# TensorE's order in the recurrence stage of a hybrid decoder layer, written by hand in pairs of tiles

## The chip, the cores and the metric

One core of one Trainium2 chip runs the whole program. The metric is the device time of one execution in microseconds (us), and the time of a kernel is the median of its runs. Engine names are those of the profile: PE is TensorE's matrix multiply, PEld its weight load, DVE is VectorE, ACT is ScalarE, POOL is GpSimd, SP is the engine that issues most DMAs.

## The reference

The layer takes x (1024 tokens by 1024 channels, float32), normalises it and multiplies it by one wide weight matrix; the columns of the product feed two branches. The attention branch scores keys with a small indexer, keeps the best 256 keys of each token (top-k), and does softmax attention over those. The recurrence branch is the part that the change touches:

```python
h = rg_lru(causal_depthwise_conv(x_rnn, conv_w, conv_b), w_rg_a, b_rg_a, w_rg_x, b_rg_x, lru_lambda)
y_rnn = (h * jax.nn.silu(g_rnn)) @ w_rnn_proj
```

where rg_lru computes, with 16 blocks of 64 channels (xb is x by blocks):

```python
r = jax.nn.sigmoid(jnp.einsum('bsgi,gij->bsgj', xb, w_a).reshape(B, S, C) + b_a)
i = jax.nn.sigmoid(jnp.einsum('bsgi,gij->bsgj', xb, w_x).reshape(B, S, C) + b_x)
log_a = -LRU_C * r * jax.nn.softplus(-lam)
a = jnp.exp(log_a)
b_in = jnp.sqrt(-jnp.expm1(2.0 * log_a)) * (i * x)
h_t = a_t * h_{t-1} + b_in_t        # an associative scan over the tokens
```

Both branches are weighted by sigmoid gates (merge), added, multiplied by w_out, added to x and normalised.

## The kernel before, in words

Everything is held with channels on the 128 partitions and tokens along the free axis, in 8 tiles of 128 channels by 1024 tokens. Each float32 operand of a product is split into a high and a low part (`split`, L93 to L95: ACT writes the high part, POOL or DVE the difference), and a product is three matrix multiplies: high by high, high by low, low by high (`proj_steps`, L115 to L125). One projection of one tile is 2 halves of 512 tokens, each 8 steps of 3 multiplies, so 48 multiplies; weights come by `load_w` (L105): two DMAs of 256 KB, then ACT and POOL split them. The accumulators of projections come from a ring of PSUM banks (`zt`); the gate products have two banks of their own (`tt`, tag "t").

The stages, in the order in which they are written:

- The score stage (L318 to L384): the indexer's scores, matrix multiplies `s`, ACT's Relu and DVE's weighting into `sc`. PE's order is written by hand there (`manual_schedule`, L357).
- The recurrence (`recurrence`, L447 to L528), for tiles of channels in the groups (0, 1), (2, 3), (4, 5), (6,), (7,). For every tile of a group: the projection `z_xr` (L478), copied to `xr` by ACT (L479); the convolution `xc`, four DVE instructions (L482, L484); the split `xs` of each half of 64 partitions, ACT and POOL (L490); the gate products `rg` of two multiplies for each half e and each 512 tokens (L495, L496), and ACT's two sigmoids of each (L499, with the time of L455). Then for every tile of the group the projection `z_gr` of the output gate, with ACT's Tanh and a DVE instruction into `sg` (L509, L510). Then the tail: ACT's Exp, Tanh, Square and Sqrt (L517 to L524), DVE's L520, L525, the scan L526 and L527, and the DMA of `u_r` to memory (L528). The helper `apart` with `turn` holds ACT's Sigmoids, Exps and Sqrts in batches, since each batch may need a table load. `xs` has one buffer for each e; `r`, `ig`, `sg`, `xc` and others have two.
- The merge gates `z_mr` of tiles 0 to 3 (L600), then the projections `z_rp` of the recurrence's result, read back as `urh` and `url` (L608 to L611), in alternation with the merge gates of tiles 4 to 7 (L612 to L622). DVE multiplies each half product into `grm` (L616).
- `topk` (L531 to L584), written after all that: a bisection of 31 rounds, each with 6 counting passes over `sc` (L541) and two tiny instructions (L551, L553), all on DVE; and at the end a chain for each of 6 blocks of rows, DVE's L579 to L583 and POOL's L584, through one buffer each of `eq` and `pre`.
- The attention stage (from L640), PE's order written by hand, in buffers that overlie those of `topk`; then the output projection.

The program is ordered by a scheduler that simulates the engines: on each engine it issues, among the instructions that it takes to be ready, the one that is written first. So before the change PE's order from L394 to L622 was the scheduler's, and it mixed the stages: `z_xr` of tile 0 between the scores, gate products between projections, `z_mr` between the gate products of tiles 6 and 7. DVE's order is the scheduler's everywhere; the counting passes of `topk`, written last, fill whatever time it believes to be free. On the chip each engine goes through its fixed order and waits where an operand is not there.

Of the kernel before, what the change touches and what calls it, by code (L numbers as in the profile page):

```python
# [18 lines left out]
P = 128  # L19
# [33 lines left out]
def hybrid_kernel(ctx: ExitStack, tc: tile.TileContext, x, w_b, w_a, w_ap, w_rp, w_o, vecs,  # L53
# [97 lines left out]
    with ExitStack() as p12:  # L151
# [295 lines left out]
        def recurrence(rn):  # L447
# [12 lines left out]
            for tiles in ((0, 1), (2, 3), (4, 5), (6,), (7,)):  # L460
                st = []
                turn()
                for c in tiles:
                    T = lambda nm, dt=F32, w=S: rn.tile([P, w], dt, tag=nm, name=f"{nm}{c}")
                    col = lambda v, c=c: vec[:, v + c:v + c + 1]

                    raw = rn.tile([P, 2, P], F32, tag="rgr", name=f"rgr{c}")
                    for e in range(2):
                        for u in range(2):
                            nc.sync.dma_start(raw[u * HD:(u + 1) * HD, e].rearrange("p (t d) -> p t d", t=2),  # L470
                                              w_rg[c, e * HD:(e + 1) * HD])
                    rgh = rn.tile([P, 2, P], F32R, tag="rgh", name=f"rgh{c}")
                    rgl = rn.tile([P, 2, P], F32R, tag="rgl", name=f"rgl{c}")
                    split(rgh, rgl, raw)
                    xr = T("xr", w=S + 3)
                    nc.gpsimd.memset(xr[:, 0:3], 0.0)
                    w = load_w(w_b[G_XR + c], f"xr{c}")
                    for c0, n, acc in proj(w, xhl, f"xr{c}"):  # L478
                        nc.scalar.activation(xr[:, 3 + c0:3 + c0 + n], acc, AF.Copy)  # L479
                    xc = T("xc")  # L480
                    cw = lambda k, c=c: vec[:, V_CW + 4 * c + k:V_CW + 4 * c + k + 1]
                    nc.vector.tensor_scalar(xc, xr[:, 0:S], cw(0), col(V_CB), op0=ALU.mult, op1=ALU.add)  # L482
                    for k in range(1, 4):
                        nc.vector.scalar_tensor_tensor(xc, xr[:, k:k + S], cw(k), xc, op0=ALU.mult, op1=ALU.add)  # L484

                    xs = [rn.tile([P, S], F32R, tag=f"xs{e}", name=f"xs{e}_{c}", bufs=1) for e in range(2)]
                    gates = [T("r"), T("ig")]
                    for e in range(2):
                        a, b = slice(e * HD, (e + 1) * HD), slice((1 - e) * HD, (2 - e) * HD)
                        split(xs[e][a], xs[e][b], xc[a])  # L490
                        bias = vec[:, V_BG + 2 * c + e:V_BG + 2 * c + e + 1]
                        for c0, n in chunks(S):
                            cs = slice(c0, c0 + n)
                            acc = tt(f"rg{c}_{e}_{c0}")
                            nc.tensor.matmul(acc, rgh[:, e], xs[e][:, cs], start=True, stop=False)  # L495
                            nc.tensor.matmul(acc, rgl[:, e], xs[e][:, cs], start=False, stop=True)  # L496
                            for u, dst in enumerate(gates):
                                f = slice(u * HD, (u + 1) * HD)
                                apart(dst[a, cs], acc[f], AF.Sigmoid, bias=bias[f])  # L499
                    r, ig = gates  # L500
                    nc.gpsimd.tensor_tensor(out=ig, in0=ig, in1=xc, op=ALU.mult)
                    st.append((c, r, ig))
# [84 lines left out]
        with ExitStack() as p3a:  # L587
# [10 lines left out]
            with tc.tile_pool(name="rn", bufs=2) as rn:  # L598
                recurrence(rn)
# [12 lines left out]
            for n in range(8):  # L612
# [8 lines left out]
                if n + 4 < 8:  # L621
                    merge_r(n + 4)  # L622
# [590 lines left out]
```

## Time and profile before

| | |
|---|---|
| time, median of 3 runs | 1211.18 us (1209.04 to 1211.36) |
| the profiled execution | 1213.4 us |
| its span, first to last instruction | 1211.5 us |
| mean granted clock of TensorE | 0.974 of full speed |

The profiled execution is 2.2 us above the median; 1.9 us of it lie around the span. All rows below are of that one execution; start times count from the beginning of its span. In a timeline row stand start, duration (both us), engine, line, operation, output<-inputs, shape and count; what the engine waited for before it stands in brackets.

### The profile page before, as it was taken

Reading aid. Unit: us, or ns where it says so; the run is one execution under the profiler, and the core shown is the slowest. Engines: PE = TensorE matmul, PEld = TensorE weight load, DVE = VectorE, ACT = ScalarE, POOL = GpSimd, SP = SyncE. Lnnn points to the kernel's source line nnn. Section 1 sums busy time; section 2 is a strip of 40 time slices with the busy share of each in tenths; the row PEclk is TensorE's granted clock in tenths of the full one; section 3 lists DMA queues with packets and bytes.
Section 4 is the critical chain, followed back from the end, with each engine's and each line's share of the span. In section 5 each row is a group of like instructions: output and inputs, shape, how many; then the busy total and the mean of one; then the engine's idle time right before and its main releaser. Section 6 shows DMA issues by size and latency. Waiting matters only on the chain.

```text
span 1211.5 us, 16044 instructions
## 1 busy us (share of the span) xinstructions
PE 1147.0 (95%) x5528; PEld 959.4 (79%) x5528; DVE 898.6 (74%) x1821; ACT 671.0 (55%) x1232; POOL 479.0 (40%) x383
## 2 busy tenths in 40 slices
PE   6989999897979899996999999999999998999997
PEld 5988878685858688885888888888888877888886
DVE  6777599999999999976776767676767698533335
ACT  6467558575668321114776777676667677332211
POOL 4211255445464422244443444444444435373000
PEclk8989999898989899997999999999999999999999
DMA  5110111111111532221001110111010231453322
GB/s 205 50 35 27 66 57 59 64 60 61 45 61 51 194 102 70 87 71 59 12 35 51 36 64 27 59 36 64 27 64 28 87 140 53 149 191 125 101 87 113
DMA packets 41665, 89.99 MB, mean 74 GB/s; under 512 B 4976, under 2 KB 8560, under 8 KB 41584
## 3 DMA queue, kind: packets, MB, share of 16 engines
q1 hardware_dynamic: 41440, 88.70, 21.6%
q8 instruction: 44, 0.72, 0.2%
q14 instruction: 37, 0.30, 0.1%
q10 hardware_dynamic: 144, 0.26, 0.1%
HBM read 68.49 MB, written 20.45 MB: 73 GB/s over the span
## 4 chain that ended last, share of the span: by engine, by line
PE 67%; DVE 21%; issue 4%; ACT 4%; DMA 2%; POOL 2%; SPq 0%; POOLq 0%; ACTq 0%; DVEq 0%
DVE junk L541 7%; PE pT L1048 4%; DVE xc L484 3%; PE o L1002 3%; PE l L844 3%; PE l L845 3%; PE f L113 2%; PE f L111 2%; PE f L112 2%; PE z_q L121 2%; PE z_rp L121 2%; PE z_q L123 2%; PE z_q L122 2%; PE z_rp L122 2%; PE z_rp L123 2%
## 5 line engine op out<-in xcount | busy, mean ns | idle before, releaser
L541 DVE TENSOR_SCALAR_CACHE_REDUCE junk<-sc,thr 128x384 bf16<-128x384 f32 (+2 forms) x192 | 181.1, 943 | 5.2
L1052 DVE TENSOR_TENSOR pp<-pT,pp 128x512 fp32r<-128x512 f32 (+1 forms) x160 | 100.8, 633 | 36.9 <-ACT pp L1051 35.2
L1051 ACT ACTIVATE pp<-pT 128x512 fp32r<-128x512 f32 (+1 forms) x160 | 87.8, 550 | 52.6 <-PE pT L1048 50.6
L844 PE MATMUL l<-kh,qt 128*128 128x128 f32 (+2 forms) x192 | 65.2, 342 | 10.4 <-POOL wlo_g L95 9.7
L1002 PE MATMUL o<-pp,vt 128*128 128x512 f32 x160 | 66.9, 418 | 2.1 <-DVE o L1017 1.0
L845 PE MATMUL l<-kl,qt 128*128 128x128 f32 (+2 forms) x192 | 66.2, 345 | 0.0
L852 ACT ACTIVATE l<-l,m 128x128 f32<-128x128 f32 (+4 forms) x80 | 54.0, 675 | 20.6 <-DVE m L846 20.3
L857 POOL TENSOR_SCALAR sc<-sc,m 128x384 f32<-128x384 f32 (+1 forms) x32 | 25.8, 805 | 92.7 <-DVE m L854 84.4
L1017 DVE TENSOR_TENSOR o<-o,o 64x256 f32<-64x256 f32 x128 | 53.4, 419 | 6.8 <-ACT o L1015 4.6
L349 ACT ACTIVATE r<-s 128x512 f32<-128x512 f32 (+1 forms) x80 | 39.8, 523 | 25.7 <-PE s L348 22.9
L354 DVE SCALAR_TENSOR_TENSOR sc<-r,wi,sc 128x384 f32<-128x384 f32 (+5 forms) x42 | 40.6, 999 | 18.0 <-ACT r L349 17.6
L121 PE MATMUL z_q<-xh,whi_q 128*128 128x512 f32 x128 | 53.6, 419 | 0.2 <-DVE kl L728 0.2
L121 PE MATMUL z_rp<-urh,whi_rp 128*128 128x512 f32 x128 | 51.4, 407 | 2.1 <-ACT urh L94 2.1
L122 PE MATMUL z_rp<-url,whi_rp 128*128 128x512 f32 x128 | 51.7, 404 | 1.5 <-DVE url L95 1.5
L852 ACT ACTIVATE sc<-sc,m 128x384 f32<-128x384 f32 (+2 forms) x48 | 44.9, 935 | 14.7 <-DVE m L846 13.4
L846 DVE CUSTOM_DVE_ANT_0 l<-sc,l 128x512 f32<-128x512 f16 (+3 forms) x80 | 41.3, 520 | 14.4 <-PE l L845 10.6
L844 PEld LDWEIGHTS l<-kh,qt 128*128 128x128 f32 x192 | 36.6, 191 | 19.4 <-POOL wlo_g L95 10.1
L854 DVE RECIPROCAL m<-m 128x1 f32<-128x1 f32 x128 | 20.3, 159 | 42.1 <-ACT l L852 22.8
L122 PE MATMUL z_gr<-xl,whi_gr 128*128 128x512 f32 x128 | 51.4, 401 | 0.0
L123 PE MATMUL z_rp<-urh,wlo_rp 128*128 128x512 f32 x128 | 51.3, 401 | 0.0
L121 PE MATMUL z_gr<-xh,whi_gr 128*128 128x512 f32 x128 | 51.3, 401 | 0.0
L1048 PE MATMUL pT<-ident,sc 128*128 128x128 f32 x288 | 48.9, 272 | 2.6 <-DVE pp L1052 2.6
(340 smaller groups left out, 3881.5 us busy)
## 6 DMA issues: line engine op xcount, KB each, us to landing
xt<-in_x_dram SPq DMA_DIRECT2D x8, 512.0 KB, 8.9
wraw_xr<-in_w_b_dram SPq DMA_DIRECT2D x16, 256.0 KB, 2.7
wraw_gr<-in_w_b_dram SPq DMA_DIRECT2D x16, 256.0 KB, 2.6
u_r<-ig SPq DMA_DIRECT2D x8, 512.0 KB, 2.9
wraw_mr<-in_w_b_dram SPq DMA_DIRECT2D x16, 256.0 KB, 3.2
wraw_rp<-in_w_rp_dram SPq DMA_DIRECT2D x16, 256.0 KB, 2.8
ur<-u_r SPq DMA_DIRECT2D x8, 512.0 KB, 3.2
wraw_q<-in_w_b_dram SPq DMA_DIRECT2D x16, 256.0 KB, 2.6
```

The lines of the kernel that those rows point to most:

```text
L121: nc.tensor.matmul(acc, wh, xh_, start=(k == 0), stop=False)
L122: nc.tensor.matmul(acc, wh, xl_, start=False, stop=False)
L123: nc.tensor.matmul(acc, wl, xh_, start=False, stop=(k == KT - 1))
L541: nc.vector.tensor_scalar(junk[:, :P * (b + 1)], SL(b), thr_of(b - B0), None, op0=op, op1=ALU.add, accum_out=cnt[:, b - B0:b - B0 + 1])
L844: nc.tensor.matmul(acc[:, :n], q, kh[:, c0:c0 + n], start=True, stop=False)
L845: nc.tensor.matmul(acc[:, :n], q, kl[:, c0:c0 + n], start=False, stop=True)
L852: nc.scalar.activation(l[:, :L], l[:, :L], AF.Exp, scale=-1.0, bias=mi, accum_out=m[:, 2:3])
L1002: nc.tensor.matmul(ov, vt[:, 2 * jj, :], pp[:, :, 0:256], start=(jj == 0), stop=False)
L1017: nc.vector.tensor_tensor(out=oc, in0=oacc[a:a + HD, u * 256:(u + 1) * 256], in1=oc, op=ALU.add)
L1048: nc.tensor.transpose(tp[:, k * P:(k + 1) * P], pr[u][:, j * P:(j + 1) * P], ident)
L1051: latest[:] = [nc.scalar.activation(pp[:, 0, :n], tp[:, :n], AF.Copy), nc.vector.tensor_tensor(out=pp[:, 1, :n], in0=tp[:, :n], in1=pp[:, ...
L1052: nc.vector.tensor_tensor(out=pp[:, 1, :n], in0=tp[:, :n], in1=pp[:, 0, :n].bitcast(F32), op=ALU.subtract)]
```

## The change

In `recurrence` the tiles go in four pairs, (6, 7) being one now. PE's instructions from the start of the recurrence to the last `z_rp` and `z_mr` are issued in the order in which they are written (`manual_schedule` for PE, closed ahead of `topk`). For a pair c, d that order is: `z_xr` of c, `z_xr` of d, `z_gr` of c with the gate products of c in it, `z_gr` of d with those of d in it. A projection has 16 steps of three multiplies; the four gate parts (two multiplies each) stand behind steps 6, 8, 10 and 12 (`run`: i is 5, 7, 9, 11). The splits `xs` of both halves are written ahead of all gate products. Then follow, as written, `z_mr` 0 to 3, and `z_rp` n with `z_mr` n + 4 behind it. The arithmetic of every tile is as before.

```diff
--- before.py
+++ after.py
@@ -457,63 +457,91 @@
             def turn():
                 before[:], since[:] = since, []
 
-            for tiles in ((0, 1), (2, 3), (4, 5), (6,), (7,)):
-                st = []
+            T = lambda nm, c, dt=F32, w=S: rn.tile([P, w], dt, tag=nm, name=f"{nm}{c}")
+            col = lambda v, c: vec[:, v + c:v + c + 1]
+            xss, rgw, gts, xcs, sgs = {}, {}, {}, {}, {}
+
+            def run(steps, amid=()):
+
+                amid = list(amid)
+                for i, _ in enumerate(steps):
+                    if i > 3 and i % 2 and amid:
+                        amid.pop(0)()
+                assert not amid
+
+            def inputs(c):
+
+                raw = rn.tile([P, 2, P], F32, tag="rgr", name=f"rgr{c}")
+                for e in range(2):
+                    for u in range(2):
+                        nc.sync.dma_start(raw[u * HD:(u + 1) * HD, e].rearrange("p (t d) -> p t d", t=2),
+                                          w_rg[c, e * HD:(e + 1) * HD])
+                rgh = rn.tile([P, 2, P], F32R, tag="rgh", name=f"rgh{c}")
+                rgl = rn.tile([P, 2, P], F32R, tag="rgl", name=f"rgl{c}")
+                split(rgh, rgl, raw)
+                rgw[c] = rgh, rgl
+                xr = T("xr", c, w=S + 3)
+                nc.gpsimd.memset(xr[:, 0:3], 0.0)
+
+                def evac(c0, n, acc):
+                    nc.scalar.activation(xr[:, 3 + c0:3 + c0 + n], acc, AF.Copy)
+
+                yield from proj_steps(load_w(w_b[G_XR + c], f"xr{c}"), xhl, f"xr{c}", evac)
+                xc = xcs[c] = T("xc", c)
+                cw = lambda k: vec[:, V_CW + 4 * c + k:V_CW + 4 * c + k + 1]
+                nc.vector.tensor_scalar(xc, xr[:, 0:S], cw(0), col(V_CB, c), op0=ALU.mult, op1=ALU.add)
+                for k in range(1, 4):
+                    nc.vector.scalar_tensor_tensor(xc, xr[:, k:k + S], cw(k), xc, op0=ALU.mult, op1=ALU.add)
+
+                for e in range(2):
+                    a, b = slice(e * HD, (e + 1) * HD), slice((1 - e) * HD, (2 - e) * HD)
+                    xs = xss[c, e] = rn.tile([P, S], F32R, tag=f"xs{e}", name=f"xs{e}_{c}", bufs=1)
+                    split(xs[a], xs[b], xc[a])
+                gts[c] = [T("r", c), T("ig", c)]
+
+            def gate_part(c, e, c0, n, last):
+                def go():
+                    rgh, rgl = rgw[c]
+                    xs = xss[c, e]
+                    a, cs = slice(e * HD, (e + 1) * HD), slice(c0, c0 + n)
+                    bias = vec[:, V_BG + 2 * c + e:V_BG + 2 * c + e + 1]
+                    acc = tt(f"rg{c}_{e}_{c0}")
+                    nc.tensor.matmul(acc, rgh[:, e], xs[:, cs], start=True, stop=False)
+                    nc.tensor.matmul(acc, rgl[:, e], xs[:, cs], start=False, stop=True)
+                    for u, dst in enumerate(gts[c]):
+                        f = slice(u * HD, (u + 1) * HD)
+                        apart(dst[a, cs], acc[f], AF.Sigmoid, bias=bias[f])
+                    if last:
+                        ig = gts[c][1]
+                        nc.gpsimd.tensor_tensor(out=ig, in0=ig, in1=xcs[c], op=ALU.mult)
+                return go
+
+            def gate_parts(c):
+                return [gate_part(c, e, c0, n, e and c0) for e in range(2) for c0, n in chunks(S)]
+
+            def out_gate(c):
+                sg = sgs[c] = T("sg", c)
+
+                def evac(c0, n, acc):
+
+                    nc.scalar.activation(sg[:, c0:c0 + n], acc, AF.Tanh, scale=0.5)
+                    nc.vector.scalar_tensor_tensor(sg[:, c0:c0 + n], sg[:, c0:c0 + n], 1.0, acc,
+                                                   op0=ALU.add, op1=ALU.mult)
+
+                return proj_steps(load_w(w_b[G_GR + c], f"gr{c}"), xhl, f"gr{c}", evac)
+
+            for tiles in ((0, 1), (2, 3), (4, 5), (6, 7)):
+                c, d = tiles
+                run(inputs(c))
+                run(inputs(d))
+                turn()
+                run(out_gate(c), gate_parts(c))
+                run(out_gate(d), gate_parts(d))
+                st2 = []
                 turn()
                 for c in tiles:
-                    T = lambda nm, dt=F32, w=S: rn.tile([P, w], dt, tag=nm, name=f"{nm}{c}")
-                    col = lambda v, c=c: vec[:, v + c:v + c + 1]
-
-                    raw = rn.tile([P, 2, P], F32, tag="rgr", name=f"rgr{c}")
-                    for e in range(2):
-                        for u in range(2):
-                            nc.sync.dma_start(raw[u * HD:(u + 1) * HD, e].rearrange("p (t d) -> p t d", t=2),
-                                              w_rg[c, e * HD:(e + 1) * HD])
-                    rgh = rn.tile([P, 2, P], F32R, tag="rgh", name=f"rgh{c}")
-                    rgl = rn.tile([P, 2, P], F32R, tag="rgl", name=f"rgl{c}")
-                    split(rgh, rgl, raw)
-                    xr = T("xr", w=S + 3)
-                    nc.gpsimd.memset(xr[:, 0:3], 0.0)
-                    w = load_w(w_b[G_XR + c], f"xr{c}")
-                    for c0, n, acc in proj(w, xhl, f"xr{c}"):
-                        nc.scalar.activation(xr[:, 3 + c0:3 + c0 + n], acc, AF.Copy)
-                    xc = T("xc")
-                    cw = lambda k, c=c: vec[:, V_CW + 4 * c + k:V_CW + 4 * c + k + 1]
-                    nc.vector.tensor_scalar(xc, xr[:, 0:S], cw(0), col(V_CB), op0=ALU.mult, op1=ALU.add)
-                    for k in range(1, 4):
-                        nc.vector.scalar_tensor_tensor(xc, xr[:, k:k + S], cw(k), xc, op0=ALU.mult, op1=ALU.add)
-
-                    xs = [rn.tile([P, S], F32R, tag=f"xs{e}", name=f"xs{e}_{c}", bufs=1) for e in range(2)]
-                    gates = [T("r"), T("ig")]
-                    for e in range(2):
-                        a, b = slice(e * HD, (e + 1) * HD), slice((1 - e) * HD, (2 - e) * HD)
-                        split(xs[e][a], xs[e][b], xc[a])
-                        bias = vec[:, V_BG + 2 * c + e:V_BG + 2 * c + e + 1]
-                        for c0, n in chunks(S):
-                            cs = slice(c0, c0 + n)
-                            acc = tt(f"rg{c}_{e}_{c0}")
-                            nc.tensor.matmul(acc, rgh[:, e], xs[e][:, cs], start=True, stop=False)
-                            nc.tensor.matmul(acc, rgl[:, e], xs[e][:, cs], start=False, stop=True)
-                            for u, dst in enumerate(gates):
-                                f = slice(u * HD, (u + 1) * HD)
-                                apart(dst[a, cs], acc[f], AF.Sigmoid, bias=bias[f])
-                    r, ig = gates
-                    nc.gpsimd.tensor_tensor(out=ig, in0=ig, in1=xc, op=ALU.mult)
-                    st.append((c, r, ig))
-                sgs = {}
-                for c, r, ig in st:
-                    w = load_w(w_b[G_GR + c], f"gr{c}")
-                    sg = sgs[c] = rn.tile([P, S], F32, tag="sg", name=f"sg{c}")
-                    for c0, n, acc in proj(w, xhl, f"gr{c}"):
-
-                        nc.scalar.activation(sg[:, c0:c0 + n], acc, AF.Tanh, scale=0.5)
-                        nc.vector.scalar_tensor_tensor(sg[:, c0:c0 + n], sg[:, c0:c0 + n], 1.0, acc,
-                                                       op0=ALU.add, op1=ALU.mult)
-                st2 = []
-                turn()
-                for c, r, ig in st:
-                    a = rn.tile([P, S], F32, tag="a", name=f"a{c}")
-                    sq = rn.tile([P, S], F32, tag="sq", name=f"sq{c}")
+                    r, ig = gts[c]
+                    a, sq = T("a", c), T("sq", c)
                     apart(a, r, AF.Exp, scale=nsp8[:, c:c + 1])
                     apart(r, r, AF.Tanh, scale=sp8[:, c:c + 1])
                     nc.scalar.activation(sq, a, AF.Square)
@@ -595,6 +623,8 @@
                     nc.scalar.activation(g[:, c0:c0 + m], acc, AF.Sigmoid,
                                          bias=vec[:, V_BM + 8 + n:V_BM + 9 + n])
 
+            by_hand = ExitStack()
+            by_hand.enter_context(tc.manual_schedule(engines={mybir.EngineType.PE}))
             with tc.tile_pool(name="rn", bufs=2) as rn:
                 recurrence(rn)
             for n in range(4):
@@ -620,6 +650,7 @@
                     nc.sync.dma_start(mr_d[n], g)
                 if n + 4 < 8:
                     merge_r(n + 4)
+            by_hand.close()
             topk(kp, kp2)
 
 
```

## Rows read from the trace of the kernel before

**Rows 1.** The page: busy time of each engine, and the chain that ended last

```profile
PE 1147.0 (95%) x5528; PEld 959.4 (79%) x5528; DVE 898.6 (74%) x1821; ACT 671.0 (55%) x1232; POOL 479.0 (40%) x383
...
PE 67%; DVE 21%; issue 4%; ACT 4%; DMA 2%; POOL 2%; SPq 0%; POOLq 0%; ACTq 0%; DVEq 0%
```

**Rows 2.** Busy time by stretch: length, engines' busy us, clock, DMA share, GB/s

```profile
120.00:147.40 27.40, 27.40 (x129) 22.75 (x129) 13.26 (x14) 14.28 (x28) 5.56 (x9) 1.00 0.20 68
...
166.42:280.00 113.58, 106.39 (x455) 86.54 (x454) 111.06 (x176) 75.36 (x100) 57.12 (x38) 0.97 0.17 56
280.00:400.00 120.00, 103.70 (x438) 84.10 (x437) 118.47 (x161) 81.22 (x104) 62.05 (x34) 0.93 0.19 64
400.00:503.00 103.00, 99.41 (x418) 79.70 (x417) 97.62 (x200) 26.46 (x37) 30.81 (x24) 0.97 0.33 111
503.00:555.40 52.40, 52.40 (x239) 42.92 (x238) 42.88 (x55) 5.50 (x10) 21.09 (x14) 1.00 0.23 79
...
166.42:555.40 388.98, 361.90 (x1544) 293.26 (x1543) 370.03 (x589) 188.55 (x251) 171.06 (x108) 0.96 0.23 76
```

**Rows 3.** Timeline of POOL, PE and DVE at the attention's start

```profile
555.52 2.40 POOL L584 TENSOR_TENSOR sc<-sc,eq 128x1024 f16<-128x1024 f32 x1 [3.74 <-DVE eq L582]
...
559.13 0.39 PE L123 MATMUL z_q<-xh,wlo_q 128*128 128x512 f32 x1
569.19 0.45 PE L844 MATMUL l<-kh,qt 128*128 128x128 f32 x1 [9.66 <-POOL wlo_g L95]
```

**Rows 4.** Waits of DVE, 166 to 556 us: total, times, longest us

```profile
DVE eq L579 <- POOL sc L584: 5.4, 4, 1.6
DVE grm L616 <- PE z_rp L123: 3.9, 4, 2.0
DVE url L95 <- ACT urh L94: 1.6, 2, 1.3
...
DVE grm L616 <- issue: 0.2, 1, 0.2
```

**Rows 5.** Waits of PE, 160 to 560 us: total, times, longest us

```profile
PE rg L495 <- issue: 15.8, 3, 8.2
PE rg L495 <- POOL xs L95: 7.7, 4, 4.9
PE z_rp L121 <- ACT urh L94: 2.1, 2, 1.8
PE z_rp L122 <- DVE url L95: 1.5, 2, 0.8
```

**Rows 6.** Timeline of PE: end of tile 3's z_xr, first gate product of tile 2

```profile
208.61 0.39 PE L122 MATMUL z_xr<-xl,whi_xr 128*128 128x512 f32 x1
...
210.20 0.39 PE L123 MATMUL z_xr<-xh,wlo_xr 128*128 128x512 f32 x1
...
228.82 0.80 PE L495 MATMUL rg<-xs,rgh 128*128 128x512 f32 x1 [4.86 <-POOL xs L95]
```

**Rows 7.** Timeline of ACT and POOL on tile 2's way to its gates; then tile 4's

```profile
204.86 0.58 ACT L479 ACTIVATE xr<-z_xr 128x512 f32<-128x512 f32 x1
...
224.87 2.14 ACT L94 ACTIVATE xs<-xc 64x1024 fp32r<-64x1024 f32 x2 [13.30 <-DVE xc L484]
...
290.45 1.08 ACT L509 ACTIVATE sg<-z_gr 128x512 f32<-128x512 f32 x2 [11.76 <-DVE ig L527]
```

**Rows 8.** z_xr on PE inside the score stage: length, busy us (count)

```profile
130.00:147.40 17.40, 9.35 (x36) 1.00 0.18 60
```

**Rows 9.** DVE's L551: all of them, two single ones, and a POOL split

```profile
L551 DVE TENSOR_SCALAR fail<-cnt 128x6 int32<-128x6 f32 x31 | 21.4, 689 | 0.7
...
244.98 2.36 DVE L551 TENSOR_SCALAR fail<-cnt 128x6 int32<-128x6 f32 x1
...
260.87 0.17 DVE L551 TENSOR_SCALAR fail<-cnt 128x6 int32<-128x6 f32 x1
...
244.92 2.40 POOL L95 TENSOR_TENSOR xs<-xc,xs 64x1024 fp32r<-64x1024 f32 x1
```

## The prediction

> **What bounds the kernel now.** I read the page first. PE is busy for 95% of the span and holds 67% of the chain that ended last, DVE 21% [rows 1]: two engines share the bound, so the place of the change must be looked at by itself. The windows come next. In the stretch from the first counting pass of topk to the end of DVE's last one, 166.42 to 555.40 us, DVE is busy 370.03 of 388.98 us and PE 361.90 [rows 2]. In the recurrence itself DVE has next to no gap (111.06 of 113.58 us, then 118.47 of 120.00), while PE has about 7 us of gaps in the first of these stretches and 16 in the second. So in the stage that is changed DVE is the fuller engine: whenever the recurrence does not need it, a counting pass of topk is in its queue.
>
> The timeline where the attention starts tells what ends this stage. PE finishes tile 0's query product at 559.5 us, then stands still for 9.66 us until the first logit at 569.19 [rows 3]. What that logit waited for came after POOL's last L584, which started at 555.52 and took 2.40 us: the end of topk. The attention's buffers lie over those of topk, so their copies and splits can only come behind it. Topk is DVE's chain. **The time is therefore set by the end of topk**, and a PE that is earlier helps only as far as DVE waits for PE. The waits of DVE say how far that is: 3.9 us in 4 waits of grm for z_rp and 0.2 us of issue [rows 4]; the 5.4 us for POOL's L584 are topk's own, and 1.6 are for ACT's urh.
>
> **The change, part by part.**
>
> *The written order of the gate products.* All 192 multiplies of a pair's four projections and the 16 of its gates stay, so PE's work stays. From 208.61 to 210.20 us are seven multiplies, 0.227 us each [rows 6], so a projection of 48 is 10.9 us. What changes is when PE stops for a gate product. The waits of PE give 23.5 us for the first multiply of a gate in all: 15.8 of "issue" and 7.7 for the split xs [rows 5].
>
> The 15.8 us are not a matter of xs. ACT stood 11.76 us ahead of tile 4's Tanh at 290.45 us, since the buffer sg had to wait for DVE's L527 of tile 2 [rows 7]; the sigmoids of the gates are queued behind that Tanh on ACT, and with two gate banks PE stops. The scheduler had run z_gr ahead of the gates, so the Tanh stood ahead of the sigmoids. In the new order the first two gate parts stand ahead of the first Tanh, and this wait can go. Its bounds are 0 and 15.8 us taken away.
>
> The 7.7 us can grow. Tile 2's gate is now written behind six steps of its z_gr: z_xr of tile 3 ended at 210.59 us, plus 18 multiplies of 0.227 is 214.7. Its xs came for 228.82 [rows 6], because ACT copied the second half of xr as late as 204.86 and got xc 13.30 us after its previous work [rows 7]: the tail of the pair before stood ahead on both engines. That is a wait of 14.1 us where there were 4.86; the scheduler's order had covered 9.3 of it with the rest of z_gr. Three pairs have a pair before them, so the bounds of this term are 0 (DVE's order follows the new order of PE) and 3 x 14.1 = 42.3 us.
>
> Together the waits lie between 0 and 42.3 us, where they were 23.5. I take 23.5, no change: DVE, 98 to 99% busy here [rows 2], paces both orders, and a PE that does not wait in one place waits in the next. What PE's waits cost the end is nothing so long as DVE is the fuller engine; the cover is topk's counting passes.
>
> *Pair (6, 7).* The tail of tiles 6 and 7 goes together, and four z_mr (4 x 10.9 = 43.6 us) now stand whole between the last gate and the first z_rp, where a part of them lay between the gate products. The waits of z_rp at its start, 2.1 us for urh and 1.5 for url [rows 5], should go, since tile 7 is no longer a turn later than tile 6. Bounds: 3.6 us taken away, or, if the last u_r comes later (no z_mr can now step in), as much added. I take 3.6 away. This lies on the path: from 503 us on PE is busy without a gap, 52.40 of 52.40 us [rows 2], and DVE waits for it 3.9 + 0.2 = 4.1 us [rows 4]. So of an earlier PE at most 4.1 us reach the end, and 3.6 fit in that.
>
> *z_xr out of the score stage.* Before, 36 multiplies of z_xr lay between 130 and 147.4 us [rows 8], 36 x 0.227 = 8.2 us, and PE had no gap from 120 to 147.4 while DVE was busy for only 13.26 of 27.4 [rows 2]: DVE waited for scores. If the written order keeps these out, scoring may end up to 8.2 us sooner, and DVE's full stretch begins sooner; or PE idles where they lay, and all later PE work moves back by as much. I take 0: PE had nothing else there, and the scores need PE's banks back from ACT.
>
> *Loads and queues.* No DMA, split or table load is added; the weights of z_gr are asked for ahead of the gates, as before, behind the same waits of SP and POOL. I cost them at nothing: the cover is a projection of 10.9 us for every load. If it is gone, each late weight would stop PE by itself, since no other product may step in.
>
> *DVE and POOL.* L551 is a tiny instruction: 0.17 us at 260.87, but 2.36 at 244.98, beside a POOL split that began at 244.92 and took 2.40 [rows 9]. All 31 took 21.4 us; 31 x 0.17 is 5.3, so 16.1 us of DVE's time is such meetings. The change moves every one of them and removes none. By the rows I take 0, with half of 16.1, so 8 us, as the bound either way. The Trainium skill, in "SBUF — State Buffer", section "Who interferes with whom", says that the two engines share a port pair, that the one that issues first holds it for its whole instruction, and that the other blocks. By that rule the new order alone could make DVE's chain longer with no work added; the row at 244.98 agrees.
>
> **The sum.** -3.6 us on the profiled execution: 1213.4 - 3.6 = 1209.8. That execution is 2.2 us above the median, so the forecast for the median is 1211.2 - 3.6 = 1207.6 us.
>
> **The rivals.**
>
> (a) *PE stops at the gates and falls behind DVE (slower).* Place: the first gate part of tiles 2, 4 and 6. Price: 42.3 us of waits for the 23.5 before, 18.8 more, less the 3.6 at z_rp: 15.2 us, 1226. For it: the way from z_xr to xs is 14.1 us too long for the written place [rows 6], and PE's slack at the end is none, since DVE's grm waits for z_rp already [rows 4]. Against: 15.8 us of PE's waits have another cause, which this order removes, and DVE's own order is planned anew. It decides as soon as PE's waits for gates exceed 23.5 + 3.6 us.
>
> (b) *Nothing at the end.* DVE's 4.1 us are merely replaced by longer waits for POOL's L584, since grm fills some of them today; or the planned order was as good as the written one. 1211.
>
> (c) *Scoring ends sooner too.* All 8.2 us of z_xr leave the score stage and DVE starts topk that much sooner: 1211.2 - 3.6 - 8.2 = 1199.4. For it: DVE's idle half there [rows 2]. Against: those multiplies were put where PE would have waited.
>
> (d) *More meetings of DVE and POOL.* The forecast with 8 us more on DVE: 1215.6. Nothing in the trace speaks for more rather than fewer.
>
> **How the numbers follow.** Forecast 0.40, (a) 0.20, (b) 0.20, (c) 0.12, (d) 0.08. A measurement of this kernel tells 0.2%, 2.4 us, from no change, so "same" is 1208.8 to 1213.6. Faster: nearly all of the forecast, (c), and a little of (b): 0.51. Same: most of (b) and the forecast's edge: 0.21. Slower: (a), (d) and a little of (b): 0.28. The forecast's own range is 1203 to 1210, the four microseconds of DVE's waits with a few of its meetings with POOL. The range to hold 8 in 10 reaches from 1198, which takes in (c), to 1221, which takes in (d) and the nearer half of (a).
>
> **What would show it.** Right: DVE as full as before up to about 500 us; grm's waits for z_rp near zero; the last L584 some 4 us earlier; the wait ahead of the first logit longer than 9.66 us. The wait of ACT's Tanh for L527 no longer ahead of a gate's "issue" wait. Wrong by (a): first gate parts of tiles 2, 4 and 6 waiting over 10 us each for xs, the last z_rp later than now, DVE's grm waiting more than 4.1 us. Wrong by (c): the first counting pass well ahead of 166.42 us. Wrong by (d): the last L584 later with DVE without gaps, and L551 above 21.4 us. The whole argument would be wrong if the first logit came earlier than topk's last instruction allows today, or if PE's later stages took another time than from 569 us on before.

## The result, and the profile after

The changed kernel takes 1220.3 us (median of 4 runs, 1219.1 to 1221.1) against 1211.3 before: a ratio of 1.0079 with a 95% interval of 1.0061 to 1.0098, so it is 9 us slower. The prediction was 1207.6, faster. The profiled execution of the changed kernel took 1221.1 us, with a span of 1219.2. In it the first logit starts 8.4 us later than in [rows 3], and what follows it takes as long as before (1219.2 - 577.6 = 641.6 us, and 1211.5 - 569.2 = 642.3). All that changed lies ahead of that logit.

The windows of the kernel after, with the columns of [rows 2]:

```profile
166.43:280.00 113.57, 96.23 (x413) 77.89 (x411) 109.06 (x169) 70.32 (x96) 58.04 (x36) 0.96 0.19 63
280.00:400.00 120.00, 108.57 (x453) 88.72 (x454) 111.39 (x169) 78.66 (x101) 60.16 (x31) 0.92 0.18 62
400.00:503.00 103.00, 94.87 (x394) 75.38 (x393) 93.11 (x191) 25.84 (x38) 32.24 (x25) 0.93 0.30 100
...
166.43:559.23 392.80, 355.90 (x1512) 287.99 (x1511) 362.78 (x589) 182.42 (x245) 168.88 (x105) 0.95 0.22 74
```

Look at the third busy column, DVE. In the last row of [rows 2] it is busy 370.0 of 389.0 us, here 362.8 of 392.8: **DVE does 7.2 us less and stands still 11.1 us more** (30.0 for 18.9). Its stretch ends 3.8 us later. PE (the first column) has more gaps than before from 166 to 280 us and again from 400 to 503, and fewer between.

The waits of PE, 120 to 580 us (total, times, longest, as in [rows 5]):

```profile
PE rg L509 <- POOL xs L95: 27.6, 4, 9.2
PE l L875 <- POOL wlo_g L95: 6.9, 1, 6.9
PE z_rp L121 <- ACT urh L94: 4.9, 2, 3.1
PE z_rp L122 <- POOL url L95: 1.6, 1, 1.6
PE z_rp L122 <- DVE url L95: 1.6, 2, 1.1
PE rg L509 <- ACT ig L455: 1.2, 1, 1.2
```

The 15.8 us of "issue" are gone, but the waits for xs rose from 7.7 to 27.6, and those of the first z_rp from 3.6 to 8.1. Three of the waits for xs are the first gate parts of tiles 2, 4 and 6 (PE's timeline; xs is the split input of a gate):

```profile
224.81 0.80 PE L509 MATMUL rg<-xs,rgh 128*128 128x512 f32 x1 [9.18 <-POOL xs L95]
...
283.42 0.79 PE L509 MATMUL rg<-xs,rgh 128*128 128x512 f32 x1 [8.15 <-POOL xs L95]
...
341.74 0.80 PE L509 MATMUL rg<-xs,rgh 128*128 128x512 f32 x1 [8.02 <-POOL xs L95]
```

The waits of DVE in the same stretch, as in [rows 4]:

```profile
DVE eq L607 <- POOL sc L612: 6.3, 5, 1.6
DVE sg L528 <- ACT sg L527: 4.6, 5, 1.4
DVE sq L553 <- ACT sq L455: 4.6, 4, 2.6
DVE grm L646 <- PE z_rp L123: 3.9, 7, 1.3
DVE url L95 <- ACT urh L94: 2.9, 3, 1.6
...
DVE sq L548 <- ACT sq L547: 0.7, 1, 0.7
```

Before, DVE waited 0.7 us for sg and not at all for sq; now it is 4.6 and 5.3 (sq is 4.6 and 0.7):

```profile
DVE sg L510 <- ACT sg L509: 0.7, 1, 0.7
```

These operands come from ACT: sg from its Tanh, sq from its Square and Sqrt. ACT in its turn now waits longer for PE's gate products, 17.7 us where it was 4.3 (waits of ACT, 195 to 400 us, before and then after; the row without a name is a table load ahead of a sigmoid):

```profile
ACT r L455 <- PE rg L496: 4.3, 7, 1.9
```

```profile
ACT r L455 <- PE rg L510: 9.1, 8, 2.4
ACT L455 <- PE rg L510: 8.6, 3, 3.0
```

So PE's stops at the gates do reach ACT. How much of DVE's added waits they make is a question for the experiments.

Where the attention starts, the timeline of DVE, POOL, SP's queue, ACT and PE reads:

```profile
559.14 0.68 DVE L646 TENSOR_TENSOR grm<-grm,z_rp 128x512 f32<-128x512 f32 x1
...
559.37 2.40 POOL L612 TENSOR_TENSOR sc<-sc,eq 128x1024 f16<-128x1024 f32 x1 [6.59 <-DVE eq L610]
561.72 2.54 POOL L95 TENSOR_TENSOR wlo_q<-wraw_q,whi_q 128x512 fp32r<-128x512 f32 x2
...
563.04 0.33 SPq L178 DMA_DIRECT2D uvr<-in_w_uv_dram  x1
563.42 0.42 SPq L648 DMA_DIRECT2D mr_d<-grm  x1
...
565.26 0.42 ACT L94 ACTIVATE uvh<-uvr 128x256 fp32r<-128x256 f32 x1 [8.99 <-PE z_q L123]
565.98 2.07 ACT L725 ACTIVATE vr<-v 128x512 f32<-128x512 f32 x4 [0.30 <-DMA mr_d<-grm]
...
570.30 0.39 PE L123 MATMUL z_q<-xh,wlo_q 128*128 128x512 f32 x1
577.57 0.44 PE L875 MATMUL l<-kh,qt 128*128 128x128 f32 x1 [6.88 <-POOL wlo_g L95]
```

Before, the same copy started as soon as POOL's L584 had ended:

```profile
557.96 2.06 ACT L694 ACTIVATE vr<-v 128x512 f32<-128x512 f32 x4 [2.27 <-POOL sc L584]
```

Topk's last POOL instruction ends 3.85 us later than in [rows 3] (561.77 for 557.92). The attention's first copy, vr, does not start there but 4.2 us later, and two things held it. A weight load (uvr) waited in SP's queue for POOL's wlo_q, which stood behind L612; on ACT the copy of that load, uvh, stood ahead of vr and ended at 565.68. And the last store of grm, ready at 559.8, stood in SP's queue behind the same load; vr waited 0.30 us more for it. So from topk's end on DVE to the first logit it is 577.57 - 559.23 = 18.34 us, where it was 569.19 - 555.40 = 13.79. The 3.83 us at topk's end and the 4.55 behind it are the 8.4.

### The profile page after: what moved, and what is told of

Read it like the earlier page. It is cut to its first block, busy times and chain, and to the rows that moved or that the text cites. A ratio compares the mean times of both kernels' runs of the same rounds, so it can differ in the third digit from the quotient of the medians.

```text
span 1219.2 us, 16042 instructions
## 1 busy us (share of the span) xinstructions
PE 1147.9 (94%) x5528; PEld 959.8 (79%) x5528; DVE 891.4 (73%) x1821; ACT 664.5 (54%) x1227; POOL 480.5 (39%) x383
## 3 DMA queue, kind: packets, MB, share of 16 engines
q1 hardware_dynamic: 41440, 88.70, 21.4%
## 4 chain that ended last, share of the span: by engine, by line
PE 47%; DVE 2%; ACT 2%; issue 1%; POOL 1%; DMA 1%; POOLq 0%; ACTq 0%; DVEq 0%
PE pT L1079 4%; PE o L1033 3%; PE l L875 3%; PE l L876 2%; PE f L112 2%; PE f L113 2%; PE f L111 2%; PE z_q L121 2%; PE z_q L122 2%; PE z_q L123 2%; PE z_g L121 2%; PE z_g L122 2%; PE z_g L123 2%; PE z_ap L123 2%; PE z_ap L122 2%; PE z_ap L121 2%
## 5 line engine op out<-in xcount | busy, mean ns | idle before, releaser
L569 DVE TENSOR_SCALAR_CACHE_REDUCE junk<-sc,thr 128x384 bf16<-128x384 f32 (+2 forms) x192 | 181.2, 944 | 5.1
L123 PE MATMUL z_gr<-xh,wlo_gr 128*128 128x512 f32 x128 | 51.4, 402 | 0.0
L122 PE MATMUL z_q<-xl,whi_q 128*128 128x512 f32 x128 | 50.8, 397 | 0.0
```

The lines of the kernel that those rows point to most:

```text
L122: nc.tensor.matmul(acc, wh, xl_, start=False, stop=False)
L123: nc.tensor.matmul(acc, wl, xh_, start=False, stop=(k == KT - 1))
L569: nc.vector.tensor_scalar(junk[:, :P * (b + 1)], SL(b), thr_of(b - B0), None, op0=op, op1=ALU.add, accum_out=cnt[:, b - B0:b - B0 + 1])
```

## The experiments

The theories were these. P: PE is late, by its stops at the gates and at the first z_rp. D: DVE's chain sets the end, and PE's lateness is only its shadow. The table has the figures that the verdicts rest on: the medians, the ratio to the kernel before as it ran in the same session, and from one profiled execution each the start of the last z_rp, the end of topk on DVE (the end of the window), DVE's busy and idle time from the first counting pass to there, and the start of the first logit.

| run | us | ratio (95%) | last z_rp | topk's end | DVE busy / idle | first logit |
|---|---|---|---|---|---|---|
| before | 1211.3 | 1 | 544.0 | 555.4 | 370.0 / 18.9 | 569.2 |
| before again (e11) | 1209.2 | one run | 541.0 | 552.4 | 367.5 / 19.9 | 566.2 |
| after | 1220.3 | 1.0079 (1.0061 to 1.0098) | 555.2 | 559.2 | 362.8 / 30.0 | 577.6 |
| after again (e12) | 1218.8 | one run | 552.2 | 556.3 | 362.6 / 28.7 | 574.8 |
| e1 | 1215.0 | 1.0041 (1.0024 to 1.0057) | 550.1 | 553.1 | 361.8 / 27.5 | 571.7 |
| e2 | 1210.8 | 1.0002 (0.9990 to 1.0014) | 537.8 | 548.2 | 353.1 / 30.3 | 562.7 |
| e3 | 1220.8 | 1.0078 (1.0059 to 1.0096) | 555.6 | 559.6 | 361.0 / 32.2 | 578.0 |
| e5 | 1211.5 | 1.0006 (0.9994 to 1.0018) | 541.3 | 553.2 | 365.9 / 22.1 | 567.0 |
| e6 | 1209.3 | 0.9986 (0.9974 to 0.9998) | 537.8 | 549.4 | 359.4 / 26.5 | 563.2 |
| e7 | 1213.3 | 1.0020 (1.0007 to 1.0033) | 554.5 | 552.9 | 355.3 / 32.5 | 570.6 |
| e8 | 1203.9 | 0.9941 (0.9919 to 0.9963) | 535.0 | 546.3 | 358.9 / 20.6 | 560.1 |
| e9 | 1216.0 | 1.0047 (1.0027 to 1.0066) | 550.8 | 554.9 | 362.2 / 27.5 | 573.3 |

Single profiled executions lie up to 4 us from their medians (that of e2 took 1207.1 us, that of before 1213.4), so a difference of less than that between two rows' start or end times says little; the waits and DVE's busy time repeat better.

One thing can be read down the table. The stretch from topk's end to the first logit is 13.8 to 14.5 us in the six rows where the last z_rp starts 10 us or more ahead of topk's end (both of before, e2, e5, e6, e8), and 18.3 to 18.6 in the five where it starts 3 to 4 us ahead of it (both of after, e1, e3, e9). So the 4.5 us behind topk's end go with a late last z_rp.

**Two executions of each kernel (e11, e12).**

> The kernel before, unchanged, profiled a second time, to see what of the split between DVE's busy and idle time is the kernel's and what is one execution's. If the meetings of DVE and POOL are fixed by the program's order, DVE's busy time between the first counting pass and topk's end is within 2 us of 370.0. If they vary from execution to execution, it differs by 3 us or more, and the total with it.

> The changed kernel, unchanged, profiled a second time. Theory (PE's waits at the gates reach DVE through ACT, and the last copies come behind a late z_rp): DVE's waits for sg and sq stay near 9 us, the last z_rp near 555 us, the stretch from topk's end on DVE to the first logit near 18 us where it was 14 before. If these were one execution's luck, they differ by 3 us or more.

The whole stretch in the windows of before again, and of after again:

```profile
165.00:552.39 387.39, 361.98 (x1544) 294.10 (x1543) 367.52 (x589) 188.46 (x250) 171.98 (x108) 0.96 0.23 76
```

```profile
164.98:556.30 391.32, 356.18 (x1512) 287.88 (x1511) 362.64 (x589) 182.33 (x245) 169.57 (x105) 0.95 0.22 74
```

DVE's busy time is 2.5 us under the first profile of before, between the 2 us and the 3 us that were to decide, and 0.1 under that of after. The first logits are 8.6 us apart, where they were 8.4. In the changed kernel DVE's waits for sg and sq are 8.6 us and the last stretch is 18.5, as expected. The picture of the two kernels holds; each was profiled only twice.

**The place of the gate parts (e2).** In the changed kernel all eight parts of a pair stand beside the second tile's z_gr:

```diff
-                    if i > 3 and i % 2 and amid:
+                    if i % 2 and amid:
...
-                run(out_gate(c), gate_parts(c))
-                run(out_gate(d), gate_parts(d))
+                run(out_gate(c))
+                run(out_gate(d), gate_parts(c) + gate_parts(d))
```

> The changed kernel, with all eight gate parts of a pair behind the odd steps of z_gr of the second tile, so those of the first tile stand 8 us of PE work later. Theory P: the three long waits of the first gate part (9.2, 8.2 and 8.0 us) fall below 2 us each, the last z_rp ends some 5 us earlier unless ACT's Tanh, which now stands ahead of the first tile's sigmoids, makes PE wait as it did before the change; time about 1215, or 1220 in that case. Rival D: the waits go, but the time stays within 2 us of 1220.

Its waits of PE:

```profile
PE rg L509 <- POOL xs L95: 8.4, 4, 3.3
PE z_rp L122 <- DVE url L95: 3.6, 3, 1.9
PE rg L509 <- ACT ig L455: 3.0, 5, 1.0
PE z_rp L122 <- POOL url L95: 2.6, 2, 1.6
PE z_rp L121 <- ACT urh L94: 2.4, 1, 2.4
PE rg L509 <- issue: 0.6, 1, 0.6
```

The waits at the gates fall from 28.8 us to 12.0, with no long wait behind a Tanh, and the time returns to that of before, lower than the 1215 that P expected: the ratio falls from 1.0079 to 1.0002. **The place of the gate parts takes the whole loss with it.** It does so on both engines at once: the last z_rp and topk's end both come earlier, and the last stretch is 14.5 us again. So this run alone does not part P from D.

But it did not do so by giving DVE its idle time back. Its window, and DVE's waits in it:

```profile
164.84:548.21 383.37, 362.45 (x1539) 289.95 (x1538) 353.11 (x589) 187.89 (x249) 167.16 (x107) 0.97 0.23 76
```

```profile
DVE eq L607 <- POOL sc L612: 8.1, 5, 2.0
DVE grm L646 <- PE z_rp L123: 6.8, 6, 1.8
DVE sq L553 <- ACT sq L455: 5.2, 3, 2.3
DVE url L95 <- ACT urh L94: 2.6, 2, 1.3
```

DVE stands idle for 30.3 us, as in the changed kernel (30.0). The waits for sg are gone (4.6 us after), those for sq are the same (5.2 for 5.3), and those for grm and eq are 4.7 us more. What is shorter is DVE's busy time, by 9.7 us. ACT, for its part, no longer waits for PE's gate products at all. So of DVE's added waits only those for sg go with the place of the gates; those for sq do not follow PE's stops there.

Where the 9.7 us come from can be worked out from the traces. Take each DVE instruction of the window and what it lasts beyond the short time of its own shape (the one that a twentieth of such instances in all runs undercut). Beside a running POOL instruction this adds up to 49.5 us before, 42.2 after, 32.2 in e2, 35.9 in e7 and 38.4 in e8; away from POOL it is 1.9 to 2.4 us in each of them. The busy times differ by DVE's meetings with POOL.

**A smaller dose (e7).** The gate parts stay beside their own tile's z_gr, but 2.7 us later:

```diff
-                    if i > 3 and i % 2 and amid:
+                    if i > 7 and i % 2 and amid:
```

> The changed kernel with the four gate parts of a tile behind steps 10, 12, 14 and 16 of its own z_gr instead of 6, 8, 10 and 12, so 2.7 us of PE work later (the second gates place moved 8 us and gave the whole loss back). If the written place is the cost, by dose: the three long first-gate waits fall by 2.7 us each, to 6.5, 5.5 and 5.3, and the time falls by a third of what 8 us gave, 2 to 4 us, to 1216 to 1218. If what helped there was something else (ACT's order of Tanh and sigmoids, or the second tile's gates), the waits fall as said but the time stays within 1 us of 1220.

```profile
PE rg L509 <- POOL xs L95: 27.4, 4, 9.6
...
PE l L875 <- PE z_q L123: 0.5, 1, 0.5
```

The waits did not fall at all, since xs came later too (tile 6's gate starts at 343.1 us instead of 341.7); the scheduler had planned DVE anew. Yet the time fell by 7 us. DVE is busy 355.3 us instead of 362.8, topk ends 6 us earlier, and the first logit now waits 0.5 us, for PE's own product. Both sides of the expectation missed. What is left in this run is PE's lateness by itself: the last z_rp is about as late as in the changed kernel, and that costs 0.2% over before, not 0.8%. The run is also a warning: most of the loss went here without PE's stops at the gates getting any shorter.

**DVE relieved (e4).** Both kernels with 27 of the 31 rounds of the bisection, so that the last four bits of each threshold are left out:

```diff
-            for k in range(30, -1, -1):
+            for k in range(30, 3, -1):
...
-                if k:
+                if k > 4:
```

> The changed kernel with 27 of the 31 rounds of topk's bisection (the last four bits of each threshold are not searched), which takes about 4 x 6.2 = 25 us of DVE's work away and no work of PE. Theory P (PE is the late one): the time falls by 3 us at most, since the last z_rp still ends at about 555 us. Rival D (DVE and topk set the end): the time falls by 8 us or more, to 1212 or below.

> The kernel before with 27 of the 31 rounds (the last four bits of each threshold are not searched), 25 us less for DVE. The premise of the prediction (DVE's chain sets the end, PE only 4 us behind it): the time falls until PE, at 559.5 us instead of 569.2, is the late one, by about 5 to 8 us, to 1203 to 1206. If PE was already the late one: it falls by 2 us at most.

The changed kernel falls to 1212.7 us (ratio 1.0021, 1.0009 to 1.0033), by 7.6, just short of the 8 that D expected and far more than P's 3; the kernel before falls to 1201.0 (0.9918, 0.9898 to 0.9939), by 10.4, more than the 5 to 8 expected. In both the first logit then waits only 0.3 us. So in both full kernels topk's end and what hangs on it set the end, as the prediction had it, and without them the time would be some 8 us (after) and 10 us (before) shorter, until PE is the late one. With DVE out of the way the changed kernel is 11.8 us the slower one, as its last z_rp is the later one (551.2 and 539.7 us in these two). P is right on where PE lost its time, D on what sets the end: PE's 11 us alone would have been covered but for 1.4 us (1212.7 against 1211.3), or 2 by e7. The other 7 or so come where the two chains meet: topk's end is later, and the copies behind it come behind a late z_rp.

**The written order behind the recurrence (e1, e3, e9).** e1 ends the written order at the recurrence:

```diff
                 recurrence(rn)
+            by_hand.close()
...
-            by_hand.close()
             topk(kp, kp2)
```

> The changed kernel, but PE's written order ends with the recurrence; z_mr and z_rp are the scheduler's again. Theory P (PE is late at the end of z_rp by 11 us, about half of it from the gate waits for xs and half from the first z_rp, which stops for urh and url where nothing may step in): the first z_rp's waits fall from 8.1 to about 3.6 us, the last z_rp ends some 4 to 6 us earlier than 555.5 us, the time is about 1215 to 1216. Rival D (DVE, with topk as its last work, sets the end; PE's lateness is only its shadow): the time stays within 2 us of 1220.

The waits of z_rp fall from 8.1 to 4.3 us and the time by 5.3 us, to 1215.0: as P expected. The waits at the gates are 28.3 us, unchanged. e3 keeps the written order and puts z_mr 4 between the steps of the first z_rp:

```diff
...
+                    side = proj_steps(load_w(w_b[G_MR + 4], "mr4"), xhl, "mr4", lambda *a: held.append(a))
+                    for _ in proj_steps(w, lambda k: (urh[:, k], url[:, k]), "rp0", mult):
+                        next(side, None)
+                        next(side, None)
...
```

> The changed kernel, with z_mr of tile 4 written between the steps of the first z_rp, two steps to one. Theory P: the waits of z_rp for urh and url fall from 8.1 to 2 us or less, PE's clock is not lowered there, the last z_rp ends 6 to 9 us earlier and the time is 1213 to 1215. Rival D: PE's waits go, the time stays within 2 us of 1220.

```profile
PE z_mr L121 <- ACT whi_mr L94: 7.5, 1, 7.5
PE z_mr L123 <- POOL wlo_mr L95: 2.9, 1, 2.9
```

The waits for urh and url are gone, but 10.4 us for the weights of z_mr 4 stand in their place, and the time is the same. The run tells nothing between the theories. e9 asks for those weights first and does half of z_mr 4 ahead:

```diff
+                w4 = load_w(w_b[G_MR + 4], "mr4") if n == 0 else None
                 w = load_w(w_rp[n], f"rp{n}")
...
+                    for _ in range(8):
+                        next(side)
+                    for _ in proj_steps(w, lambda k: (urh[:, k], url[:, k]), "rp0", mult):
+                        next(side, None)
...
```

> The changed kernel with half of z_mr 4 ahead of the first z_rp and the other half between its first eight steps, and the weights of z_mr 4 asked for before those of z_rp (the run without that only moved the wait to z_mr's weights: 7.5 and 2.9 us). If PE's waits at the first z_rp are 5 of the 9 us: waits for urh and url fall from 8.1 to 3 us or less with no new wait for weights, the last z_rp ends by 550.5 us and the time is 1214 to 1217. If they cost nothing: within 2 us of 1220.

There are no waits for urh and url, but, against the expectation, 3.6 and 2.9 us of new ones for the weights of z_rp; the last z_rp starts at 550.8 us and the time falls to 1216.0, inside the range. So the order behind the recurrence is worth 4 to 5 us of the changed kernel's time.

**Both repairs (e8).** The edits of e1 and e2 together:

> Both repairs at once: all eight gate parts beside z_gr of the second tile, and PE's written order only over the recurrence. If the two losses are apart (gate place 9 us, order of z_mr and z_rp 5 us), the time is 1205 to 1207 and beats the kernel before by 0.4%. If DVE alone bounds what is left, it stays within 2 us of 1210.8.

```profile
166.85:546.29 379.44, 361.54 (x1542) 289.85 (x1541) 358.87 (x589) 188.24 (x250) 169.74 (x108) 0.98 0.23 77
```

1203.9 us, ratio 0.9941 (0.9919 to 0.9963): **faster than both kernels**, by a little more than expected. DVE's idle time is 20.6 us, 9 less than after and near that of before, and it is busy 11 us less than before. Writing the recurrence's order by hand in pairs can pay; the place of the gates and the reach of the written order decide.

The changed kernel, e1, e2 and e8 are the four combinations of two choices. Later gate parts give 0.77% under the long written order (after to e2) and 1.00% under the short one (e1 to e8); the short order gives 0.38% with early gate parts (after to e1) and 0.61% with late ones (e2 to e8). So each of the two gives time by itself. How it reaches DVE differs: from e1 to e8 DVE's idle time falls by 6.9 us and its busy time by 2.9; from after to e2 the idle time stays and the busy time falls by 9.7.

**Parts acquitted (e5, e6).** e5 is the kernel before with the last two tiles as a pair:

```diff
-            for tiles in ((0, 1), (2, 3), (4, 5), (6,), (7,)):
+            for tiles in ((0, 1), (2, 3), (4, 5), (6, 7)):
```

> The kernel before, with tiles 6 and 7 as one pair and nothing else changed, so that the scheduler still orders PE. If pairing the last two tiles costs time by itself (the tail of both comes late together), the time rises by 3 us or more over 1211 and the first z_rp waits over 6 us. Theory P (it is the written order that costs): within 2 us of 1211.

1.0006: pairing costs nothing by itself. e6 gives the kernel before a third sg buffer, and one buffer instead of two to the raw gate weights, to make room:

```diff
-raw = rn.tile([P, 2, P], F32, tag="rgr", name=f"rgr{c}")
+raw = rn.tile([P, 2, P], F32, tag="rgr", name=f"rgr{c}", bufs=1)
...
-sg = sgs[c] = rn.tile([P, S], F32, tag="sg", name=f"sg{c}")
+sg = sgs[c] = rn.tile([P, S], F32, tag="sg", name=f"sg{c}", bufs=3)
```

> The kernel before with three buffers for sg (and one for the raw gate weights, to make room), so that the Tanh of a pair does not wait for the scan of the pair before and the sigmoids behind it do not stop PE: some 15 us of PE's 23.5 us of gate waits should go. If DVE alone sets the end: time within 3 us of 1211. If PE's waits count for themselves: 1200 to 1206.

ACT's timeline beside tile 4's gates:

```profile
275.97 0.58 ACT L509 ACTIVATE sg<-z_gr 128x512 f32<-128x512 f32 x1
...
290.79 1.26 ACT L455 ACTIVATE ig<-rg,vec 64x512 f32<-64x512 f32 x2 [11.66 <-DVE sg L510]
```

The Tanh no longer waits, but a sigmoid behind it waits 11.66 us for DVE. Its output ig has two buffers as well, and both belonged to the pair before, for DVE's scan and the store of u_r; that it waits for these is read from the code, not shown. PE's "issue" waits stay at 14.2 us, so the run did not take away what it was meant to; the time moved by 0.14%. What PE's waits cost the kernel before is not settled by it.

## Why the prediction was wrong, point by point

*What bounds the stage.* Right for the kernel before: without 4 rounds of topk it falls by 10.4 us, until the first logit hardly waits, and the slack in [rows 3] is 9.66.

*The gates.* This is the first step that failed. The prediction took PE's waits at the gates as 23.5 us in both kernels, since "DVE paces both orders, and a PE that does not wait in one place waits in the next", and held that such waits cost nothing so long as DVE is the fuller engine. The waits became 28.8 us. The 15.8 of "issue" went, as the order of Tanh and sigmoid had promised; the three first gate parts waited 9.2, 8.2 and 8.0 us, against 14.1 as the bound. PE reached tile 2's gate at 215.6 us, near the forecast 214.7, but xs came at 224.8 and not at 228.8. The upper bound of 42.3 us for all these waits left out the case that the 15.8 stay; with them it is 58.1.

And the waits were not free. Moving the gate parts gave 0.77% back (e2), more than the 0.38% of the order behind the recurrence (e1). Two ways of it can be told apart. One is shown: the last z_rp comes 11 us later, and the copies behind topk's end come 4.5 us later with it. The other is DVE's chain. The counting passes were named as the cover, but DVE's order is fixed ahead, and it stops at sg and sq with counting passes behind them:

```profile
254.36 0.69 DVE L528 SCALAR_TENSOR_TENSOR sg<-sg,z_gr 128x512 f32<-128x512 f32 x1 [1.38 <-ACT sg L527]
254.96 0.74 DVE L569 TENSOR_SCALAR_CACHE_REDUCE junk<-sc,thr 128x512 bf16<-128x512 f32 x1
```

The first pass of the same round (L569) had run at 252.35 us, so the threshold of this one was there. DVE's idle time rose by 11.1 us, 9.2 of them for sg and sq. Which part of that is PE's stops handed on by ACT stays open: the waits for sg go when the gate parts move (e2), the waits for sq and the sum of DVE's idle time do not.

*Pair (6, 7).* This step failed too. The prediction took 3.6 us of waits away; they became 8.1, 4.5 more. Tile 7's last DVE instruction did start 4 us earlier (391.1 for 395.5), but the url tiles still arrive one by one until 425.6 us, and before the scheduler had filled such gaps with z_mr 4. The bound "or as much added" was near; the wrong end was chosen. e5 shows that it is not the pairing, e1 and e9 that it is the order, worth 4 to 5 us of the time.

*z_xr out of the score stage.* Zero was right, for another reason than given: nothing left. The same 36 multiplies lie there after as before (z_xr on PE, as in [rows 8], where the row gives them 9.35 us and the prediction reckoned 8.2):

```profile
130.00:147.40 17.40, 9.24 (x36) 1.00 0.17 60
```

*DVE and POOL.* The bound of 8 us either way held: DVE was busy 7.2 us less, the good side. Rival (d) is out. The prediction cited the Trainium skill, "SBUF — State Buffer", section "Who interferes with whom", for a port pair that one of the two engines holds for its whole instruction while the other waits (the page says for which kinds of DVE instruction). The traces agree so far: with the same instructions in another order, DVE's busy time moved from 370.0 to as little as 353.1 us (e2), and nearly all of the time that its instructions take beyond their short time lies beside POOL's.

*The last stretch* was taken as fixed behind topk's end. It grew by 4.5 us, since copies and loads that used to be done by then come behind the late z_rp and queue behind one another.

*The sum* by the profiled execution: 11.07 us more idle and 7.25 less busy are 3.8 at topk's end, and with 4.55 behind it that is 8.4, where -3.6 was forecast. Rival (a), the written order stopping PE at the gates, came nearest, at 9 us instead of 15.2. Of its signs the later z_rp came; first gate waits over 10 us each and longer waits of grm for z_rp did not (9.2 at most, and 3.9 as before). Its price left out that PE had 9.66 us of slack, and the loss came by the end of topk and the copies behind it, not by PE directly. Its chance of 0.20 was too low: the 14.1 us that the trace already showed for tile 2 were outweighed by a general argument about DVE.

What stays open is why DVE meets POOL so much less in e2 and e7 than in the changed kernel. Each edit made the scheduler plan DVE anew, and no run moved the gate parts with DVE's order held, so a part of what they gave back may be that new order and not PE's shorter stops.

## What to carry to other kernels

A product that is written into another engine's stream at a fixed place needs its operand there by the trace of the chip, the late engines' queues included: count from the last producer to the consumer in the trace and put the product behind that (here 8 us of other work later turned a loss of 0.8% into none, though 2.7 us later, with the stops as long as ever, already left only 0.2%). A full engine covers a stall only with what stands ahead in its own order: here DVE, 95% busy before, went from 18.9 to 30.0 us idle often with counting passes standing behind the waiting instruction. And end a written order where arrival times begin to vary, so that a planner can fill the gaps (4 to 5 us here).

## What the runs showed of the hardware that was not expected

DVE's busy time for the same work, 589 instructions, depends on the order more than on the execution. It repeats within 0.1 us for the changed kernel and 2.5 for the one before, each profiled twice, but spreads from 353.1 to 370.0 us over orders. The 31 instances of the tiny L551 (L579 after the change) show it: 21.4 and 21.5 us in the two profiles of before, 18.7 and 17.1 in those of after, 12.8 in e7. Here are the second of before and e7:

```profile
L551 DVE TENSOR_SCALAR fail<-cnt 128x6 int32<-128x6 f32 x31 | 21.5, 693 | 0.7
```

```profile
L579 DVE TENSOR_SCALAR fail<-cnt 128x6 int32<-128x6 f32 x31 | 12.8, 414 | 0.8
```

So an edit that only moves instructions can change DVE's busy time by more than the forecast effect of this change. The time need not follow: in e6 DVE is busy 10.6 us less than before, stands idle about 7.5 us more, and the time moved by 0.14%.
